# Sixteen instead of twelve row tiles of the down projection by seven products, weight low parts by adding DMA transfers, token-tile-major finish, and stacked rotary scores

## The chip, the cores and the metric

One core of a Trainium2 chip runs the whole program. The metric is device time in microseconds (us) of one execution; a measurement is the median of several. The engines named below are TensorE (PE: matrix products; its weight loads are a row of their own, PEld), VectorE (DVE), ScalarE (ACT), GpSimd (POOL), SyncE (SP, which here only issues DMA transfers), and the 16 DMA engines of the core.

## The reference

Two layers of a decoder on 512 tokens with 1024 features, all in float32. Per layer, with `swiglu(x) = (silu(x @ w_gate) * (x @ w_up)) @ w_down` and 2816 hidden columns:

```python
x = LN1(alpha * x + 0.5 * swiglu_1(x))
x = LN2(alpha * x + mixer(x))        # gated DeltaNet + conformer convolution + latent attention
x = LN3(alpha * x + 0.5 * swiglu_2(x))
```

The attention inside the mixer has four heads; a score is the sum of a part without position (128 wide) and a rotary part (64 wide, its key shared by the heads):

```python
s = (einsum('bqhd,bkhd->bhqk', q_nope[:, q0:q1], k_nope[:, :q1])
     + einsum('bqhr,bkr->bhqk', q_rope[:, q0:q1], k_rope[:, :q1])) * scale
```

## The kernel before

**Products in three passes.** A float32 matrix is split into a high part `h` (the value rounded to the type float32r, by a ScalarE copy) and a low part `lo = value - h` (by a VectorE subtraction): `split_into`. A product of two split matrices is three TensorE instructions, high by high, high by low and low by high (`mm3`). Products of two unsplit float32 matrices exist too, each of which appears in the trace as two instructions.

**Seven products instead of eight.** For a block product of two by two blocks the kernel uses a scheme with seven block products and some additions (`seven` for the gate and up projections, `seven_out` for the down projection). In the down projection the contraction has 22 row tiles of 128. `DOWN_FAST = 6` pairs of them (12 row tiles) go through `seven_out`: 7 products x 2 token tiles x 3 = 42 instructions of 512 columns a pair, where the direct way (`acc`) takes 2 x 8 x 3 = 48. `seven_out` walks over the pairs three times: a pass into the banks `x` and `y` (12 instructions a pair), one into `v`, `x`, `y` (18), one into `z`, `v` (12). The other 10 row tiles are done directly: a loop over the two halves of the output columns (`hf`), and in each over weights (`load`) and the four token tiles `tt` of 128 tokens; the last `TAIL = 5` weights of the second half are held, so that the token tiles end one after the other, 30 instructions apart. After its second half a token tile is normalised (`Norm.half`, `Norm.finish`), written out, and turned into the `xh`, `xl` of the next stage (`to_features`).

**Buffers.** Weights land in one of `RAWS = 5` buffers (`raw`), whose next load waits until its last reader is done; their split parts and sums of weights lie in slots, of which weights may hold 28 of 76.

**Order.** Each operation is recorded first, and `Planner.plan` then sets the order of all engines at build time from costs, due times (`prio`) and free buffers. On the chip each engine runs its list in that order and waits by semaphores.

**Rotary scores.** The rotary queries of two heads lie in one tile (`qr[h // 2]`), the shared key in two tiles, each with zeros in one half (`kropes`, two memsets by GpSimd). A score block of n columns is two unsplit float32 products, `qn` by `kn` and `qr` by `kropes`, with n = 128, 256, 384 and 512.

## Time and profile before

| | |
|---|---|
| runs | 2416.09, 2416.36, 2418.67 us; median 2416.36 |
| profiled execution | 2416.95 us, its span from the first to the last instruction 2415.2 us |
| busy | PE 2390.1, DVE 2215.7, ACT 1328.2, POOL 2.3 us |
| granted TensorE clock | 0.999 of full speed (2.4 GHz) |

A busy PE is not PE at its peak, since the end of a matmul is modelled; how densely it works is read from the count of matmuls of one shape in a stretch. The profile puts every operation on one line (288, the end of the planner), so operations are told apart by engine, shape and the names of what they write and read (`s` a slot, `ps` a bank of products, `raw` a weight buffer). The four down projections lie at about 226 to 353, 1098 to 1210, 1438 to 1551 and 2293 to 2406 us.

### The profile page before, as it was taken

The numbers are of one execution on the slowest core, as the hardware profiler recorded it, in microseconds if no ns is written. First come the engines' busy times: TensorE is split into PE (matmuls) and PEld (weight loads), VectorE is DVE, ScalarE is ACT, GpSimd is POOL, SyncE is SP. The second block draws the span as 40 slices with busy tenths as digits, with TensorE's granted clock in tenths as the row PEclk, the third lists the DMA queues.
The fourth block names the chain that finished last, engine by engine and source line by source line (L and its number), as shares of the span: only waits on it lengthen the run. The fifth ranks groups of instructions, "written<-read, shape, count | busy, mean of one in ns | idle before, by whom it ended". The sixth has DMA issues, their size and how long they took to land.

```text
span 2415.2 us, 41549 instructions
## 1 busy us (share of the span) xinstructions
PE 2390.1 (99%) x15716; PEld 2179.4 (90%) x15716; DVE 2215.7 (92%) x4559; ACT 1328.2 (55%) x2901; POOL 2.3 (0%) x8
## 2 busy tenths in 40 slices
PE   8999999999999999999999999999999999999998
PEld 8999888888899899998899998888888998999986
DVE  8998987999999799989799999789999997999896
ACT  6555538536746545656356565294376464555561
POOL 0000000000000000000000000000000000000000
PEclk9999999999999999999999999999999999999999
DMA  5334562412333623334523345523123335233451
GB/s 167 106 109 153 162 180 71 106 50 69 89 104 97 209 68 108 106 109 162 183 88 106 106 155 173 169 56 98 40 83 92 104 105 183 88 105 106 147 160 70
DMA packets 269833, 280.33 MB, mean 116 GB/s; under 512 B 18676, under 2 KB 221632, under 8 KB 269632
## 3 DMA queue, kind: packets, MB, share of 16 engines
q1 hardware_dynamic: 269632, 277.67, 38.3%
q8 instruction: 123, 2.02, 0.3%
q14 instruction: 78, 0.64, 0.1%
HBM read 260.33 MB, written 17.30 MB: 115 GB/s over the span
## 4 chain that ended last, share of the span: by engine, by line
PE 86%; DVE 7%; ACT 4%; DMA 1%; issue 1%; SPq 0%; DVEq 0%; ACTq 0%
PE ps L288 86%; DVE s L288 7%; ACT s L288 3%; ACT ps L288 1%; DMA raw<-in_ffn_w_up 0%; ACT xh L288 0%; DMA raw<-in_w_in 0%; DMA raw<-in_cv_w_pw 0%; DMA s<-in_x 0%; DMA raw<-in_ffn_w_gate 0%; DVE lny L288 0%; DVE xl L288 0%; DVE lnt L288 0%; DMA xspill<-s 0%; DVE cst L288 0%
## 5 line engine op out<-in xcount | busy, mean ns | idle before, releaser
L288 PE MATMUL ps<-s 128*128 128x256 f32 (+3 forms) x9068 | 1518.3, 323 | 1.4 <-DVE s L288 1.0
L288 PEld LDWEIGHTS ps<-s 128*128 128x128 f32 x9068 | 1324.9, 190 | 140.9 <-issue 5.7
L288 PE MATMUL ps<-xh,s 128*128 128x256 f32 (+2 forms) x4064 | 900.4, 307 | 1.5 <-ACT s L288 1.2
L288 DVE TENSOR_TENSOR s<-s 128x512 fp32r<-128x512 f32 (+9 forms) x1254 | 711.9, 600 | 4.3 <-ACT s L288 2.2
L288 PEld LDWEIGHTS ps<-xh,s 128*128 128x128 f32 (+1 forms) x4064 | 678.5, 190 | 34.8 <-ACT s L288 1.6
L288 PE MATMUL ps<-xl,s 128*128 128x256 f32 (+2 forms) x2032 | 624.6, 308 | 0.0
L288 DVE TENSOR_TENSOR s<-raw,s 128x512 fp32r<-128x512 f32 (+1 forms) x844 | 548.5, 679 | 11.9 <-ACT s L288 11.5
L288 ACT CAST s<-raw 128x512 fp32r<-128x512 f32 (+1 forms) x716 | 422.4, 619 | 220.7 <-DMA raw<-in_ffn_w_down 69.5
L288 ACT CAST s<-s 128x512 fp32r<-128x512 f32 (+1 forms) x786 | 436.3, 594 | 188.3 <-DVE s L288 179.1
L288 ACT COPY s<-ps 128x256 f32<-128x256 f32 (+3 forms) x664 | 257.2, 401 | 343.3 <-PE ps L288 336.1
L288 PEld LDWEIGHTS ps<-xl,s 128*128 128x128 f32 (+1 forms) x2032 | 387.0, 190 | 16.6 <-DVE xl L288 0.2
L288 DVE SCALAR_TENSOR_TENSOR s<-s 128x512 f32<-128x512 f32 (+26 forms) x356 | 249.9, 713 | 2.8 <-ACT s L288 2.1
L288 DVE TENSOR_TENSOR s<-ps,s 128x256 f32<-128x256 f32 (+1 forms) x336 | 147.4, 439 | 66.6 <-PE ps L288 53.8
L288 DVE TENSOR_TENSOR s<-raw 128x512 f32<-128x512 f32 x256 | 173.4, 682 | 5.1 <-issue 3.2
L288 ACT ACTIVATE s<-s 128x512 f32<-128x512 f32 x162 | 103.0, 666 | 59.6 <-DVE s L288 57.1
L288 PE MATMUL ps<-ident,s 128*128 128x128 f32 (+1 forms) x508 | 86.0, 277 | 12.6 <-DMA s<-in_x 5.0
L288 ACT CAST xh<-ps 128x512 fp32r<-128x512 f32 x48 | 28.6, 596 | 126.6 <-PE ps L288 126.6
L288 PEld LDWEIGHTS ps<-ident,s 128*128 128x128 f32 (+1 forms) x508 | 60.8, 142 | 32.2 <-issue 13.0
L288 DVE TENSOR_TENSOR s<-s,raw 128x512 f32<-128x512 f32 x128 | 87.2, 682 | 0.0
L288 DVE SCALAR_TENSOR_TENSOR s<-s,ps 128x512 f32<-128x512 f32 x96 | 63.4, 681 | 21.8 <-PE ps L288 18.9
L288 DVE TENSOR_TENSOR s<-s,ps 128x512 f32<-128x512 f32 x76 | 50.6, 680 | 32.4 <-PE ps L288 32.4
L288 ACT ACTIVATE s<-ps,s 128x512 f32<-128x512 f32 x58 | 40.3, 715 | 50.2 <-PE ps L288 50.2
(101 smaller groups left out, 599.3 us busy)
## 6 DMA issues: line engine op xcount, KB each, us to landing
raw<-in_w_in SPq DMA_DIRECT2D x106, 512.0 KB, 3.8
raw<-in_ffn_w_down SPq DMA_DIRECT2D x88, 512.0 KB, 4.4
raw<-in_ffn_w_gate SPq DMA_DIRECT2D x80, 512.0 KB, 3.8
raw<-in_ffn_w_up SPq DMA_DIRECT2D x80, 512.0 KB, 3.8
raw<-in_ffn_w_down SPq DMA_DIRECT2D x48, 256.0 KB, 2.6
spill<-s SPq DMA_DIRECT2D x40, 256.0 KB, 2.0
s<-spill SPq DMA_DIRECT2D x40, 256.0 KB, 4.7
raw<-in_w_out SPq DMA_DIRECT2D x16, 512.0 KB, 5.2
```

What stands on the lines that cost most here:

```text
L288: self.issued = o["f"](*o["a"], **o["k"])
```

## The change

In the down projections `DOWN_FAST` goes from 6 to 8 pairs (16 of 22 row tiles). The low part of a weight that came straight from memory is no longer subtracted by VectorE: ScalarE writes the negated value in float32r, and a GpSimd DMA adds the weight buffer to it (`split_adding`), for the first pass from pair `ADDING_FROM = 2` on, for all others and for the directly multiplied weights: 6 + 8 + 8 + 12 = 34 transfers of 256 KB in each down projection, 136 in all. Sums of weights (`t1`, `t3`, `t2`) are split as before. The directly multiplied rest is now a loop over token tiles outside and column halves inside, with all its weights held; the third pass leaves out the `v` products of the last `DOWN_LATE = 4` pairs, and these (`last`) come after token tile 1. The planner gets a cost for such a DMA. In the rotary scores, a query's split parts are stacked in the two halves of one tile per head, and the key's high and low part (each in both halves) are two float32r products of at least 256 columns.

```diff
+        if engine == "POOL" and name == "dma_start":
+            return 1200.0
...
+        if engine == "POOL" and name == "dma_start":
+            lat = 7000.0
...
-TAIL = 5
-DOWN_FAST = 6
+DOWN_FAST = 8
+DOWN_LATE = 4
+ADDING_FROM = 2
...
+        def split_adding(h, lo, part, src):
+
+            S.copy(h, part)
+            S.mul(lo, part, -1.0)
+            G.dma_start(out=lo.bitcast(F32), in_=src, accum_op=ADD)
...
-                split_into(h, lo, part)
+                if adding is None:
+                    split_into(h, lo, part)
+                else:
+                    split_adding(h, lo, part, part)
...
-            banks = seven_out(norm, wsrc, a32, fast) if fast else {}
+            if fast:
+                banks, last = seven_out(norm, wsrc, a32, fast, late)
+                norm.load()
+                rest = range(fast, n // 2)
+                ws = [[load(hf, fp, True) for fp in rest] for hf in range(2)]
+                for f in range(2 * fast, n):
+                    prepare(f)
+                for tt in range(NT):
+                    if tt == 2:
+                        last()
+                    for hf in range(2):
+                        old = (tt, hf) in banks
+                        ps = banks[tt, hf] if old else bank("dn")
+                        for fp, w in zip(rest, ws[hf]):
+                            for j in range(2):
+                                acc(ps, tt, 2 * fp + j, w, j, fp + j == fast and not old, old)
+                        norm.half(tt, hf, ps)
+                    norm.finish(tt)
+                return
...
-                product(x, halves(op, LO), wsplit(b11), i)
+                product(x, halves(op, LO), wsplit(b11, src if i >= ADDING_FROM else None), i)
...
-                product(y, s4, wsplit(b22), i, True)
+                product(y, s4, wsplit(b22, src), i, True)
...
-                t4 = slot(F32, WEIGHTS)
-                V.tensor_tensor(t4, b21, t2[i], op=SUB)
-                product(z, halves(op, LO), wsplit(b21), i)
-                product(v, halves(op, HI), wsplit(t4), i, True)
+                V.tensor_tensor(t2[i], b21, t2[i], op=SUB)
+                product(z, halves(op, LO), wsplit(b21, src), i)
+                if i < n - late:
+                    product(v, halves(op, HI), wsplit(t2[i]), i, True)
+                held.append(op)
+
+            def last():
+                for i in range(n - late, n):
+                    product(v, halves(held[i], HI), wsplit(t2[i]), i, True)
...
-            kr2 = slot()
-            G.memset(kr2[0:64], 0.0)
-            V.tensor_copy(kr2[64:128], krope[64:128])
-            G.memset(krope[64:128], 0.0)
-            kropes = krope, kr2
+            krope = split(rope(kr, swapped(kr_sb, (0, 0))))
...
-                qr.append(rope(t, swapped(ps, (0, 64))))
+                t = rope(t, swapped(ps, (0, 64)))
+                for i in range(2):
+                    q = slot(F32R)
+                    mine, other = slice(64 * i, 64 * i + 64), slice(64 - 64 * i, 128 - 64 * i)
+                    split_into(q[mine], q[other], t[mine])
+                    qr.append(q)
...
-                    PE.matmul(ps[:, 0:n], lhsT=qn[h][:, c], rhs=kn[h][:, 0:n], start=True, stop=False)
-                    PE.matmul(ps[:, 0:n], lhsT=qr[h // 2][:, c], rhs=kropes[h % 2][:, 0:n], start=False, stop=True)
+                    m = max(n, 256)
+                    for part in range(2):
+                        PE.matmul(ps[:, 0:m], lhsT=qr[h][:, c], rhs=krope[part][:, 0:m], start=part == 0, stop=False)
+                    PE.matmul(ps[:, 0:n], lhsT=qn[h][:, c], rhs=kn[h][:, 0:n], start=False, stop=True)
```

The change moves instructions at three places that matter below. The planner's end is line 288 before and line 292 after, so equal rows differ in that number.

ScalarE while the first down projection's first and second pass over the pairs are fed, before (`CAST s<-raw` is the high part of a loaded weight, `CAST s<-s` that of a sum or of hidden values):

```order
L288 CAST s<-s 128x512 x4
L288 CAST s<-raw 128x512
L288 CAST s<-s 128x512 x3
L288 CAST s<-s 128x256
L288 CAST s<-s 128x512
L288 CAST s<-raw 128x512
L288 CAST s<-s 128x512 x7
L288 CAST s<-s 128x256
L288 CAST s<-raw 128x512
```

The same engine at the same stage of the change:

```order
L292 CAST s<-raw 128x512
L292 ACTIVATE s<-raw 128x512
L292 CAST s<-s 128x512 x3
L292 CAST s<-s 128x256
L292 CAST s<-s 128x512
L292 CAST s<-s 128x256
L292 CAST s<-raw 128x512
L292 ACTIVATE s<-raw 128x512
L292 CAST s<-s 128x512 x2
```

Behind the cast of a loaded weight there is now a second pass over the same buffer, the negation (`ACTIVATE s<-raw`).

GpSimd's whole list from the last constant on, before:

```order
L1397 MEMSET const-bfloat16-1.0 128x1
L1397 MEMSET const-uint8-127 128x1
L1401 UNCONDITIONAL_BRANCH
L288 MEMSET s 64x512 x4
L1401 UNCONDITIONAL_BRANCH
L1397 ISA
```

and in the change:

```order
L1441 MEMSET const-bfloat16-1.0 128x1
L1441 MEMSET const-uint8-127 128x1
L1445 UNCONDITIONAL_BRANCH
L292 DMA s<-raw 128x512 x136
L1445 UNCONDITIONAL_BRANCH
L1441 ISA
```

The four memsets of the rotary keys are gone and 136 adding transfers have come, one behind the other in one queue that holds nothing else.

TensorE at the end of the first down projection and the start of the mixer, before (`ident,s 128x128` are the transposes that hand a normalised token tile to the next stage, `xh,s 72x256` is the first product of the mixer, `s 128x512` the down projection):

```order
L288 MATMUL ps<-s 128x512 x423
L288 MATMUL ps<-ident,s 128x128 x4
L288 MATMUL ps<-s 128x512
L288 MATMUL ps<-ident,s 128x128 x4
L288 MATMUL ps<-s 128x512 x33
L288 MATMUL ps<-ident,s 128x128 x4
L288 MATMUL ps<-s 128x512
L288 MATMUL ps<-ident,s 128x128 x4
L288 MATMUL ps<-s 128x512 x29
L288 MATMUL ps<-xh,s 72x256
```

and in the change:

```order
L292 MATMUL ps<-s 128x512 x433
L292 MATMUL ps<-ident,s 128x128 x4
L292 MATMUL ps<-s 128x512
L292 MATMUL ps<-ident,s 128x128 x4
L292 MATMUL ps<-s 128x512 x15
L292 MATMUL ps<-ident,s 128x128 x4
L292 MATMUL ps<-s 128x512
L292 MATMUL ps<-ident,s 128x128 x4
L292 MATMUL ps<-s 128x512 x23
L292 MATMUL ps<-xh,s 72x256
```

Behind the second token tile's last transposes there are now 23 instead of 29 instructions of the down projection, behind the first tile's 39 instead of 63. The two other tiles are handed over among the first products of the mixer: the third behind 35 of them, where it was behind 7.

## Rows read from the trace of the kernel before

**Rows 1.** The page's first part: busy us of each engine, its share of the span and its number of instructions.

```profile
PE 2390.1 (99%) x15716; PEld 2179.4 (90%) x15716; DVE 2215.7 (92%) x4559; ACT 1328.2 (55%) x2901; POOL 2.3 (0%) x8
```

**Rows 2.** The page's fourth part: the chain of work that ended last, its share of the span by engine.

```profile
PE 86%; DVE 7%; ACT 4%; DMA 1%; issue 1%; SPq 0%; DVEq 0%; ACTq 0%
```

**Rows 3.** The table of stretches: stretch, its length, then busy us (and instructions) of each engine, granted clock, share of the DMA engines, GB/s. The first three lie in the first layer's mixer, the fourth in a down projection, the fifth in a gate and up projection.

```profile
680.00:720.00 40.00, 40.00 (x287) 37.84 (x286) 40.00 (x70) 19.23 (x38) 0.00 (x0) 1.00 0.34 100
720.00:760.00 40.00, 39.50 (x268) 36.36 (x268) 38.27 (x81) 25.71 (x48) 0.00 (x0) 1.00 0.36 106
760.00:800.00 40.00, 40.00 (x293) 38.05 (x292) 37.55 (x67) 24.80 (x49) 0.00 (x0) 1.00 0.32 93
...
1120.00:1160.00 40.00, 40.00 (x178) 33.10 (x177) 40.00 (x69) 20.91 (x38) 0.00 (x0) 1.00 0.53 164
1360.00:1400.00 40.00, 40.00 (x336) 40.00 (x335) 35.55 (x64) 22.91 (x48) 0.00 (x0) 1.00 0.36 106
```

**Rows 4.** The timeline of the last down projection: start, us, engine, line, operation, count; in brackets the idle time before it and what ended that. The last two rows are the first and the last VectorE work behind the last matmul.

```profile
2344.64 61.36 PE L288 MATMUL ps<-s 128*128 128x512 f32 x270
...
2359.96 4.89 DVE L288 TENSOR_TENSOR s<-raw,s 128x512 fp32r<-128x512 f32 x8
...
2406.03 0.69 DVE L288 TENSOR_TENSOR s<-s,ps 128x512 f32<-128x512 f32 x1 [0.71 <-PE ps L288]
...
2410.70 1.41 DVE L288 SCALAR_TENSOR_TENSOR s<-s,lny 128x512 f32<-128x512 f32 x2
```

**Rows 5.** The timeline of TensorE in the mixer: unsplit float32 products (128 wide first, then score products of 384 and 512 columns) and what follows each.

```profile
540.88 14.90 PE L288 MATMUL ps<-s 128*128 128x128 f32 x132
555.53 0.48 PE L288 MATMUL ps<-xl,s 128*128 128x512 f32 x1
...
609.52 1.46 PE L288 MATMUL ps<-s 128*128 128x384 f32 x4
610.81 0.49 PE L288 MATMUL ps<-ident,s 128*128 128x128 f32 x3
611.14 1.88 PE L288 MATMUL ps<-s 128*128 128x512 f32 x4
612.86 0.60 PE L288 MATMUL ps<-ident,s 128*128 128x128 f32 x4
```

**Rows 6.** Groups of instructions with shapes kept apart: count, busy us in total, mean ns of one, idle us before them.

```profile
L288 DVE TENSOR_TENSOR s<-raw,s 128x512 fp32r<-128x512 f32 x700 | 459.3, 682 | 11.9 <-ACT s L288 11.5
...
L288 ACT CAST s<-raw 128x512 fp32r<-128x512 f32 x700 | 415.2, 622 | 219.0 <-DMA raw<-in_ffn_w_down 69.5 <-DMA raw<-in_w_in 43.9 <-DMA raw<-in_ffn_w_gate 38.5
...
L288 ACT ACTIVATE s<-s 128x512 f32<-128x512 f32 x162 | 103.0, 666 | 59.6 <-DVE s L288 57.1 <-DVE gu L288 1.8
...
L288 DVE TENSOR_TENSOR s<-s 128x256 f32<-128x256 f32 x100 | 38.4, 416 | 0.1
```

**Rows 7.** The page's sixth part: DMA issues with count, size of one and median us from issue to landing; and the landing times of all loads of the down projection's weights.

```profile
raw<-in_ffn_w_down SPq DMA_DIRECT2D x88, 512.0 KB, 4.4
...
raw<-in_ffn_w_down SPq DMA_DIRECT2D x48, 256.0 KB, 2.6
spill<-s SPq DMA_DIRECT2D x40, 256.0 KB, 2.0
s<-spill SPq DMA_DIRECT2D x40, 256.0 KB, 4.7
...
DMA to landing us min/median/max: 2.4/4.0/8.8
```

**Rows 8.** The table of stretches, as in rows 3, for the first down projection.

```profile
226.00:246.00 20.00, 20.00 (x140) 18.70 (x139) 17.38 (x33) 13.64 (x29) 0.00 (x0) 1.00 0.66 213
246.00:266.00 20.00, 20.00 (x90) 16.57 (x89) 20.00 (x37) 14.86 (x28) 0.00 (x0) 1.00 0.52 167
266.00:286.00 20.00, 19.04 (x85) 15.42 (x84) 20.00 (x36) 10.12 (x19) 0.00 (x0) 1.00 0.30 91
286.00:306.00 20.00, 20.00 (x90) 16.45 (x89) 19.50 (x35) 10.47 (x19) 0.00 (x0) 1.00 0.77 246
306.00:326.00 20.00, 20.00 (x90) 16.57 (x89) 15.33 (x27) 9.29 (x17) 0.00 (x0) 1.00 0.80 216
```

**Rows 9.** The waits of the DMA issuing queue of SyncE: who was waited for, us in total, times, longest.

```profile
SPq L288 <- DVE s L288: 1988.2, 485, 33.9
```

**Rows 10.** The timeline of TensorE where the down projections of the two first feed-forward blocks hand over to the mixers: every matmul that waited.

```profile
356.06 0.63 PE L288 MATMUL ps<-ident,s 128*128 128x128 f32 x4 [1.74 <-DVE s L288]
363.54 0.63 PE L288 MATMUL ps<-ident,s 128*128 128x128 f32 x4 [0.24 <-DVE s L288]
...
1553.91 0.63 PE L288 MATMUL ps<-ident,s 128*128 128x128 f32 x4 [0.33 <-DVE s L288]
1561.38 0.63 PE L288 MATMUL ps<-ident,s 128*128 128x128 f32 x4 [0.24 <-DVE s L288]
```

**Rows 11.** The chain of work that ended last, in order of time, in the first mixer: start, us, what (`cst` are the statistics of the convolution branch); and the wait of TensorE at its end.

```profile
593.09 100.99 PE ps L288 x611
...
734.96 1.22 DVE cst L288 x2
...
747.38 119.82 PE ps L288 x728
747.38 0.55 PE L288 MATMUL ps<-ident,s 128*128 128x128 f32 x3 [0.50 <-ACT s L288]
```

More of the change, by code (lines that the diff above doesn't have):

```diff
@@ L163, in _record @@
         lat = {"SP": 2000.0, "PE": 200.0, "ACT": 140.0, "DVE": 160.0, "POOL": 180.0}[engine]
+        if engine == "POOL" and name == "dma_start":
+            lat = 7000.0
         sb = [x for x in ins if x.space == bass.MemoryType.SB and (x.free_size() > 1 or outs[0].free_size() == 1)]
-        port = engine == "POOL" and bool(sb) or engine == "DVE" and (
+        port = engine == "POOL" and name != "dma_start" and bool(sb) or engine == "DVE" and (
             len(sb) > 1 or name in ("tensor_scalar", "tensor_copy") and len(sb) == 1 and outs[0].space == bass.MemoryType.SB)
@@ L407, in split_into, with weight @@
             (eng or V).tensor_tensor(lo, src, h.bitcast(F32), op=SUB)
-        def weight(shape, pieces, hold=False, biases=None):
+        def split_adding(h, lo, part, src):
+            S.copy(h, part)
+            S.mul(lo, part, -1.0)
+            G.dma_start(out=lo.bitcast(F32), in_=src, accum_op=ADD)
+        def weight(shape, pieces, hold=False, biases=None, adding=None):
             raw = pl.tile(wraw_p, shape, F32, "raw", RAWS)
@@ L429, in block, with wblock @@
             return src.rearrange("(k p) c -> p k c", p=128)
-        def wblock(src, hold=False):
+        def wblock(src, hold=False, adding=False):
             s = block(src)
-            return weight(list(s.shape), [(ALL, s)], hold)
+            return weight(list(s.shape), [(ALL, s)], hold, adding=s if adding else None)
         def wblock_first(src, i):
@@ L548, in trunk, with token_out @@
         LO, HI = slice(0, 256), slice(256, 512)
-        def token_out(norm, wsrc, n, ah, al, tail, prepare=None, a32=None, fast=0):
+        def token_out(norm, wsrc, n, ah, al, a32=None, fast=0, late=0, tail=0, prepare=None):
             def load(hf, fp, hold=False):
-                return wblock(wsrc[fp * 256:(fp + 1) * 256, hf * 512:(hf + 1) * 512], hold)
+                return wblock(wsrc[fp * 256:(fp + 1) * 256, hf * 512:(hf + 1) * 512], hold, fast > 0)
             def acc(ps, tt, f, w, j, first, more):
@@ L577, in token_out @@
                             f = n - 2 * rest + 2 * i + j
-                            acc(ps[tt], tt, f, w, j, f == 2 * fast and not old[tt], old[tt])
+                            acc(ps[tt], tt, f, w, j, f == 0, False)
                     norm.half(tt, hf, ps[tt])
@@ L581, in token_out, with seven_out @@
                         norm.finish(tt)
-        def seven_out(norm, wsrc, a32, n):
+        def seven_out(norm, wsrc, a32, n, late):
             pairs = [(i, n + i) for i in range(n)]
@@ L588, in rows, with wsplit @@
                 raw = pl.tile(wraw_p, [128, m], F32, "raw", RAWS)
-                Q.dma_start(out=raw, in_=wsrc[f * 128:(f + 1) * 128, cols])
-                return [raw[:, c:c + 512] for c in range(0, m, 512)]
-            def wsplit(w):
+                src = wsrc[f * 128:(f + 1) * 128, cols]
+                Q.dma_start(out=raw, in_=src)
+                return [(raw[:, c:c + 512], raw[:, c:c + 512]) for c in range(0, m, 512)]
+            def wsplit(w, src=None):
                 h, lo = slot(F32R, WEIGHTS), slot(F32R, WEIGHTS)
-                split_into(h, lo, w)
+                if src is None:
+                    split_into(h, lo, w)
+                else:
+                    split_adding(h, lo, w, src)
                 return h, lo
@@ L608, in seven_out @@
             for i, (f, g) in enumerate(pairs):
-                b11, b12 = rows(f)
+                (b11, src), (b12, _) = rows(f)
                 s = slot()
@@ L623, in seven_out @@
             for i, (f, g) in enumerate(pairs):
-                (b11, b12), (b22,) = rows(f), rows(g, slice(512, 1024))
+                (b11, _), (b12, _) = rows(f)
+                (b22, src), = rows(g, slice(512, 1024))
                 s = s23[i]
@@ L788, in ffn @@
             residual(src)
-            token_out(Norm(g[l], b[l], 4 * ALPHA, 16 * EPS, then), wd, NF, hh, hl, TAIL, prepare, hid, DOWN_FAST)
+            norm = Norm(g[l], b[l], 4 * ALPHA, 16 * EPS, then)
+            token_out(norm, wd, NF, hh, hl, hid, DOWN_FAST, DOWN_LATE, 0, prepare)
         def rope_setup():
@@ L1368, in mixer @@
             norm = Norm(a["ln2_g"][l], a["ln2_b"][l], 2 * ALPHA, 4 * EPS, "ffn")
-            token_out(norm, a["w_out"][l], 8, [m[0] for m in merged], [m[1] for m in merged], TAIL_OUT)
+            token_out(norm, a["w_out"][l], 8, [m[0] for m in merged], [m[1] for m in merged], tail=TAIL_OUT)
         for tt in range(NT):
```

15 lines of the change are left out of this document (6 added, 9 removed).

## The prediction

> **What bounds the kernel now.** First the busy times: PE 2390.1 of 2415.2 us, VectorE 2215.7, ScalarE 1328.2 [rows 1]. The chain that ended last is TensorE for 86% of the span and VectorE for 7% [rows 2], so TensorE is the bound and VectorE is close behind. A busy TensorE is not yet a dense one, so next the stretches: a down projection holds 178 matmuls of 512 columns in 40.00 us, a gate and up projection 336 of 256 columns [rows 3]. Over the whole last down projection it is 61.36 us for 270, 0.227 us each [rows 4], and 40.00 / 336 = 0.119 us for 256 columns. The spacing goes with the column count and nothing is left between: in these stages the time is the number of TensorE instructions, and an instruction less is time less, as long as VectorE, ScalarE and the transfers still deliver. VectorE is full there too, 20.00 of 20.00 us from 246 to 286 [rows 8], and in the mixer 40.00 of 40.00 [rows 3].
>
> **Down projection.** A pair through seven products costs 42 instructions instead of 48. Two more pairs in each of four down projections: 2 x 6 x 4 = 48 instructions fewer, 48 x 0.227 = **10.9 us**. All other products are moved, not changed.
>
> Whether the feeders keep up, per pair. By the code VectorE does, before, 4 full subtractions and 2 of 256 columns in the first pass, 6 and 3 in the second, 4 in the third. A full one takes 4.89 / 8 = 0.61 us [rows 4], a half one 38.4 / 100 = 0.38 us [rows 6]: 14 x 0.61 + 5 x 0.38 = 10.4 us, against 42 x 0.227 = 9.5 us of TensorE. For 8 pairs that is 83 against 76 us: without help VectorE would be late by some 7 us, minus what it has prepared. The change takes three full subtractions of each pair away (for two pairs, two): 8 x 10.4 - 22 x 0.61 = 70 us, below 76. ScalarE gets the negations. It then makes 13 full passes and one half pass a pair at 415.2 / 700 = 0.59 us [rows 6], about 8.0 us, below 9.5; up to 0.67 us each, the dearest such pass (`ACTIVATE`) [rows 6], it is 9.0 us. ScalarE is at 14.86 of 20 us in its fullest stretch there [rows 8]. So I put both at nothing, covered by TensorE's own 9.5 us a pair; without that cover it would be the 7 us above per down projection.
>
> **The adding transfer.** GpSimd was nearly idle (2.3 us [rows 1]), so no row shows a transfer issued there, nor one that adds. What stands behind it: its queue has only these 136, in the order in which ScalarE makes them ready; behind each landing wait TensorE's second product of three (high by low) and the reuse of the weight buffer. The second matters more, since SP's queue already spends 1988.2 us waiting for VectorE to let go of a buffer [rows 9], and now it waits for the landing instead. Call the time from issue to landing L. In the first pass a pair uses one of the five buffers and 12 x 0.227 = 2.72 us of TensorE; five make a turn of 13.6 us. The load takes 4.4 us [rows 7], cast and negation 1.2 us, which leaves L = 8.0 us before the ring sets the pace. In the third pass the load takes 2.6 us [rows 7], and 8 pairs use 4 x 2.72 + 4 x 1.36 = 16.3 us of TensorE, a mean turn of 10.2 us: L = 6.4 us. The second pass has two buffers per pair and 18 x 0.227 = 4.1 us, and leaves more. Bounds for L: 2.0 us, the shortest median of 256 KB (a store), and 8.8 us, the longest landing of any load of these weights [rows 7]. I take 4.7 us, that of the 256 KB loads which come in bunches [rows 7], since the adding transfers run between weight loads. Then nothing waits; at 8.8 us the two passes lose 8 x (5.6 + 8.8) / 5 - 21.8 + 8 x (3.8 + 8.8) / 5 - 16.3 = 5 us in each down projection, 20 us in all.
>
> The DMA engines: 213 GB/s at a share of 0.66 and 216 at 0.80 [rows 8] put a full engine set at some 300 GB/s (an estimate), so 256 KB cost 0.9 us once and 1.75 us if the read of the target counts too. 34 of them are 30 to 60 us in a stage of 480 x 0.227 = 109 us; the stage's own weights, now 15.7 MB, need 52 us. Together 82 to 112 us: it fits, at the upper end only just.
>
> **Finish by token tiles.** Before, TensorE waited 1.74, 0.24, 0.33 and 0.24 us for VectorE where the first feed-forward blocks hand over to the mixer [rows 10]. In the order now the third tile's transposes stand 35 products after the down projection's end instead of 7, 28 x 0.12 = 3.4 us later, and the last two tiles are 36 x 0.227 = 8.2 us apart, not 30 x 0.227 = 6.8. I take **2.0 us** of these 2.55; nothing if another wait comes instead, and at most 3 us. At the end of the kernel the tail stays: 2406.03 to 2410.70 and on [rows 4] hangs on the last matmul only.
>
> **Rotary scores.** An unsplit product shows as two instructions. 128 columns: (555.53 - 540.88) / 132 = 0.111, so 0.22 us a product; 384: (610.81 - 609.52) / 4 x 2 = 0.645; 512: (612.86 - 611.14) / 4 x 2 = 0.86 [rows 5]; 256, half of that, 0.43. A head drops 0.22 + 0.43 + 0.645 + 0.86 = 2.16 us, eight heads 17.3 us. New are two split products each of 256, 256, 384 and 512 columns: 2 x (0.12 + 0.12 + 0.17 + 0.227) = 1.27 us, for eight heads 10.2. That is **7.1 us** less for TensorE. VectorE gets four low parts of 64 rows and one of 128 a layer and loses a copy, about +2.7 us; ScalarE five casts, about 3 us, which its 19.23 of 40 us covers [rows 3]. VectorE has no cover in the mixer: it is full until 720, and the convolution's statistics at 734.96 end its run, after which TensorE waits 0.50 us [rows 11]. The planner's order answers that: counted in it with these durations, VectorE has 18.7 us more ahead of the statistics (gate work brought forward), and TensorE 18.2 us more ahead of the transposes that they need. So this wait grows by about 0.5 us a layer; I charge 1.0 us.
>
> **Sum**, against the profiled execution of 2416.95 us (span 2415.2): 2416.95 - 10.9 - 2.0 - 7.1 + 1.0 = 2397.95 us. The median of the runs lies 0.6 below that execution, which is less than I can tell: **2398 us**.
>
> **Rivals.** (a) *VectorE sets the mixer.* Its 2.7 us a layer come on top and the 7.1 us are waited away at the convolution: 2398 + 6.1 + 5.4 = 2409.5 us. For it: both engines are at 40.00 of 40.00 [rows 3]. Against: from 760 on VectorE has 2.45 us free in 40 [rows 3], and the order moves work into the gap.
>
> (b) *The adding transfers land late*, in the first and third pass. The loss per down projection is 3.2 x L - 23 us; it eats the 19 us gained at L = 8.7 us, and at L = 10 us it is 9 us, the kernel then 2398 + 36 = 2434 us. For it: loads of these weights took up to 8.8 us [rows 7], and the DMA engines come near to full. Against: 256 KB usually need 2.0 to 4.7 us.
>
> (c) *VectorE keeps GpSimd from issuing.* If a transfer could start only where VectorE pauses, and VectorE works 70 of 76 us, L would grow by several us, to the 2434 us of (b). For it: 20.00 of 20.00 us [rows 8]. Against: no row shows the two engines in each other's way. The Trainium skill (SBUF — State Buffer, Who interferes with whom) has such a lock: a VectorE copy or tensor_scalar in a two-port mode shuts GpSimd out of writing descriptors until it ends, while a subtraction of two buffers is said to clash with GpSimd's reads alone. By that page the subtractions that fill this stage would hold nothing up; no run here shows it yet.
>
> (d) *The gain is larger*: handovers and the mixer's starts lose their waits too, some 8 us more: 2390 us.
>
> **Chances.** The forecast (2390 to 2405 us) 0.62; (a), 2405 to 2411, 0.13; (d), below 2390, 0.05; (b) 0.15, of which 0.06 lies within no change and 0.09 above; (c) 0.05. A measurement tells apart 0.2%, 4.8 us. Faster than 2411.5 us: 0.62 + 0.13 + 0.05 = 0.80. The same: 0.06. Slower: 0.09 + 0.05 = 0.14. The range is 2389 to 2418 us, which leaves out about 0.05 below and 0.14 above; the likeliest case alone is 2390 to 2405.
>
> **What would show it.** Right: 178 matmuls in 40 us still within the down projections, and some 2.7 us less for each; landing of the GpSimd transfers at 3 to 6 us; score products at 0.12 to 0.23 us; the wait at the convolution below 2 us. Wrong: TensorE waiting in the down projection for a DMA with `s<-raw`; SP waiting for these transfers rather than for VectorE with the loads late behind; GpSimd's issues more than 2.7 us apart in the first pass; a VectorE chain ending in the convolution's statistics with a long TensorE wait behind it.

## The result and the profile after

The changed kernel takes 2450.36 us (median of 4 runs, 2442.59 to 2455.78), the kernel before beside it 2417.52: a ratio of 1.0130, 95% interval 1.0118 to 1.0143. The prediction was 2398 us; the change costs 33 us instead of gaining 19. The profiled execution lasts 2450.15 us, its span is 2448.4 (before 2415.2, [rows 1]).

The page's first part, its third (queue: packets, MB, share of 16 DMA engines), and one row of its sixth (DMA issues, median us to landing), of the kernel after:

```profile
PE 2393.4 (98%) x15668; PEld 2177.6 (89%) x15668; DVE 2188.0 (89%) x4535; ACT 1423.3 (58%) x3087; POOL 117.5 (5%) x140
...
q1 hardware_dynamic: 269888, 281.87, 38.1%
q0 software_dynamic: 19584, 35.66, 8.3%
...
s<-raw POOLq DMA_DIRECT2D x136, 256.0 KB, 6.2
...
PE 38%; DVE 7%; DMA 5%; ACT 2%; issue 1%; POOL 0%; DVEq 0%; SPq 0%; ACTq 0%; POOLq 0%
```

TensorE is still "busy" for 98%, and VectorE has lost work as planned (2215.7 to 2188.0). The chain of the work that ended last (last row, fourth part of the page) can be followed back only to 1156.8 us, so that its shares add up to 53% of the span: of that part TensorE has 38 in 53, or 72% (86% before, of a chain over nearly the whole span [rows 2]), and DMA, 1% before, has 5 in 53. GpSimd's queue takes 8.3% of the DMA engines' span: 8.3% of 2448.4 us by 136 is 1.49 us of all sixteen engines for one 256 KB adding transfer.

**Where the time went.** From the start times of the matmuls, the us from the first to the last product of 512 columns of each down projection, and of what lies between (a handover ends at the first product of 512 columns behind the mixer's 72 by 72 transposes):

| stretch | before | after | passes only | passes, ring of 7 |
|---|---|---|---|---|
| four down projections | 117.4, 116.2, 116.1, 114.2 | 130.5, 124.2, 126.9, 116.4 | 120.7, 117.2, 118.7, 113.4 | 122.2, 113.4, 113.8, 111.5 |
| handovers to the mixers | 21.9, 20.5 | 23.1, 20.0 | 19.9, 19.9 | 19.9, 20.0 |
| down to down of the next block | 224.7 | 225.2 | 223.8 | 224.4 |
| mixers, up to the next down | 720.3, 718.6 | 716.5, 721.1 | 718.1, 719.0 | 715.5, 716.4 |

The last two columns are experiments, below. In the changed kernel the down projections take 498.0 us for 463.9, where 480 products of 0.227 us would be 109 each. That is the whole loss (+34.1); the mixers give 1.3 back.

The table of stretches over the four down projections, kernel before, then after (stretch, length, busy us of PE, PEld, DVE, ACT, POOL with counts, granted clock, DMA share, GB/s):

```profile
226.00:353.00 127.00, 126.04 (x614) 106.16 (x613) 115.80 (x223) 67.19 (x125) 0.00 (x0) 1.00 0.60 181
1095.00:1220.00 125.00, 124.92 (x604) 105.02 (x603) 112.30 (x217) 63.07 (x118) 0.00 (x0) 1.00 0.48 155
1435.00:1560.00 125.00, 124.67 (x604) 104.95 (x603) 111.86 (x223) 60.33 (x115) 0.00 (x0) 1.00 0.57 172
2291.00:2406.00 115.00, 115.00 (x521) 95.43 (x519) 97.04 (x187) 45.76 (x86) 0.00 (x0) 1.00 0.38 120
```

```profile
226.00:353.00 127.00, 117.33 (x546) 97.44 (x545) 93.88 (x179) 82.62 (x157) 29.42 (x34) 0.96 0.97 241
1095.00:1220.00 125.00, 118.38 (x560) 98.51 (x559) 93.89 (x180) 82.66 (x157) 29.33 (x34) 0.97 0.95 246
1435.00:1560.00 125.00, 118.83 (x601) 100.29 (x600) 90.04 (x159) 84.37 (x162) 29.28 (x34) 0.99 0.93 233
2291.00:2406.00 115.00, 112.25 (x622) 97.98 (x621) 93.89 (x166) 81.45 (x158) 25.87 (x30) 0.99 0.86 225
```

In the first one the DMA engines were at 0.60 and are at 0.97. In us of all engines: 0.60 x 127 = 76 before, and 34 x 1.49 = 51 more make 127 of 127. The losses (13, 8, 11 and 2 us) stand in the order of the shares before: the fourth down projection had 0.38 (no next block's weights are loaded beside it), and it lost least. That the full average is itself the cause does not follow; an experiment below speaks against it.

Within the first one, ten us at a time, after:

```profile
266.00:276.00 10.00, 10.00 (x46) 8.28 (x45) 6.86 (x13) 5.93 (x12) 1.72 (x2) 1.00 0.83 239
...
296.00:306.00 10.00, 9.94 (x44) 8.25 (x45) 10.00 (x18) 7.13 (x13) 3.04 (x5) 1.00 1.01 256
306.00:316.00 10.00, 6.95 (x28) 5.06 (x27) 5.87 (x10) 6.57 (x13) 4.31 (x6) 0.96 1.01 264
316.00:326.00 10.00, 4.44 (x14) 3.18 (x13) 0.00 (x0) 1.18 (x3) 1.66 (x2) 0.84 1.10 271
326.00:336.00 10.00, 9.82 (x31) 7.85 (x32) 0.32 (x1) 6.59 (x13) 5.16 (x6) 0.69 1.13 231
336.00:346.00 10.00, 10.00 (x46) 8.29 (x45) 7.42 (x13) 3.97 (x8) 0.00 (x0) 1.00 1.16 270
```

(The share sums the packets that begin in a stretch, so it can pass 1.00.) Up to 306 TensorE is nearly dense (41 to 46 products in 10 us from 246 on). Then, in the third pass and ahead of the late weight blocks (those of the directly multiplied rest, six of 512 KB), TensorE and ScalarE stop, and VectorE has nothing to do (0.00 and 0.32 us): no engine is the bound, the transfers are. Before it can issue the next load, SP's queue waited for VectorE there (104.3 us from 280 to 400 in the kernel before); now it waits about as long for landings as for VectorE (us in total, times, longest):

```profile
SPq L292 <- DVE s L292: 41.9, 15, 16.9
SPq L292 <- DMA s<-raw: 40.6, 13, 5.9
```

The stop also costs clock: from 316 to 326 TensorE worked for 4.44 us, and from 326 to 336 it is busy again, but at a granted 0.69 (a mean of its two levels, 1.2 and 2.4 GHz) it makes 31 products for 46.

The chain in the second down projection, in order of time (start, us, what):

```profile
1169.39 6.73 DMA raw<-in_ffn_w_down
...
1176.70 14.44 DMA raw<-in_ffn_w_down
...
1192.69 0.83 POOL s L292
...
1193.70 7.09 DMA s<-raw
...
1200.91 0.37 SPq L292
...
1201.33 4.90 DMA raw<-in_ffn_w_gate
```

The load of a late block, 512 KB, whose like took 4.4 us before [rows 7], stands in the chain for 14.44; its low part is then added in 7.09, and only behind that landing does SP issue loads of the next block's weights. The engines in between show it too (ScalarE's timeline: its first cast of the late block ahead of that one, then its first cast of that one, each with the idle time before it):

```profile
1187.79 0.62 ACT L292 CAST s<-raw 128x512 fp32r<-128x512 f32 x1 [7.37 <-DMA raw<-in_ffn_w_down]
...
1191.22 0.62 ACT L292 CAST s<-raw 128x512 fp32r<-128x512 f32 x1 [1.24 <-DMA raw<-in_ffn_w_down]
```

### The profile page after: what moved, and what is told of

It is laid out like the page before. It is cut to its first block, busy times and chain, and to the rows that moved or that the text cites. A ratio compares the mean times of both kernels' runs of the same rounds, so it can differ in the third digit from the quotient of the medians.

```text
span 2448.4 us, 42105 instructions
## 1 busy us (share of the span) xinstructions
PE 2393.4 (98%) x15668; PEld 2177.6 (89%) x15668; DVE 2188.0 (89%) x4535; ACT 1423.3 (58%) x3087; POOL 117.5 (5%) x140
## 3 DMA queue, kind: packets, MB, share of 16 engines
q1 hardware_dynamic: 269888, 281.87, 38.1%
q0 software_dynamic: 19584, 35.66, 8.3%
## 4 chain that ended last, share of the span: by engine, by line
PE 38%; DVE 7%; DMA 5%; ACT 2%; issue 1%; POOL 0%; DVEq 0%; SPq 0%; ACTq 0%; POOLq 0%
PE ps L292 38%; DVE s L292 6%; ACT s L292 2%; DMA raw<-in_ffn_w_down 2%; DMA raw<-in_w_in 1%; DMA s<-raw 1%; DMA raw<-in_ffn_w_gate 0%; DMA raw<-in_w_out 0%; ACT ps L292 0%; DMA raw<-in_ffn_w_up 0%; DMA raw<-in_dn_w_o 0%; DVE st L292 0%; POOL s L292 0%; DVE lny L292 0%; DVE lnt L292 0%
## 5 line engine op out<-in xcount | busy, mean ns | idle before, releaser
L292 PE MATMUL ps<-s 128*128 128x256 f32 (+2 forms) x9020 | 1518.1, 324 | 28.3 <-ACT s L292 13.8
L292 DVE TENSOR_TENSOR s<-s 128x512 fp32r<-128x512 f32 (+9 forms) x1344 | 757.6, 598 | 4.8 <-ACT s L292 1.3
L292 ACT CAST s<-raw 128x512 fp32r<-128x512 f32 x708 | 423.4, 620 | 264.1 <-DMA raw<-in_w_in 71.5
L292 ACT CAST s<-s 128x512 fp32r<-128x512 f32 (+1 forms) x844 | 466.8, 591 | 163.6 <-DVE s L292 155.1
L292 DVE TENSOR_TENSOR s<-raw,s 128x512 fp32r<-128x512 f32 (+1 forms) x708 | 459.8, 678 | 21.9 <-ACT s L292 21.3
L292 DVE SCALAR_TENSOR_TENSOR s<-s 128x512 f32<-128x512 f32 (+27 forms) x356 | 250.9, 713 | 1.8 <-ACT s L292 0.9
L292 POOL DMA_DIRECT2D s<-raw x136 | 117.3, 865 | 2295.3 <-ACT s L292 2228.7
L292 DVE TENSOR_TENSOR s<-raw 128x512 f32<-128x512 f32 x272 | 184.5, 682 | 16.1 <-DMA raw<-in_ffn_w_down 7.5
L292 DVE TENSOR_TENSOR s<-s,raw 128x512 f32<-128x512 f32 x136 | 92.6, 681 | 0.0
L292 ACT ACTIVATE s<-raw 128x512 fp32r<-128x512 f32 x136 | 85.3, 627 | 0.0
```

Of the source, the lines that this page charges most:

```text
L292: self.issued = o["f"](*o["a"], **o["k"])
```

## The experiments

All are timed against the kernel before on the same chip.

| run | us | ratio (95%) |
|---|---|---|
| changed kernel | 2450.4 | 1.0130 (1.0118 to 1.0143) |
| stacked scores alone | 2415.2 | 0.9989 (0.9980 to 0.9997) |
| changed, no adding transfer | 2428.9 | 1.0043 (1.0031 to 1.0055) |
| adding in the passes only | 2417.1 | 0.9993 (0.9983 to 1.0002) |
| adding in the late blocks only | 2463.5 | 1.0188 (1.0175 to 1.0201) |
| passes only, finish by halves | 2426.4 | 1.0038 (1.0025 to 1.0050) |
| changed, seven raw buffers | 2435.4 | 1.0076 (1.0063 to 1.0088) |
| changed, plain transfers | 2411.6 | 0.9978 (0.9968 to 0.9988) |
| adding in passes one and two | 2419.7 | 1.0016 (1.0006 to 1.0026) |
| scores, no more VectorE work | 2419.1 | 1.0006 (0.9997 to 1.0015) |
| **passes only, seven raw buffers** | **2404.6** | **0.9949 (0.9936 to 0.9963)** |
| passes one and two, seven buffers | 2420.9 | 1.0015 (1.0006 to 1.0024) |
| scores alone, seven buffers | 2422.3 | 1.0016 (1.0008 to 1.0025) |
| scores, casts on GpSimd | 2416.0 | 0.9993 (0.9984 to 1.0002) |
| passes only, seven, casts on GpSimd | 2404.8 | 0.9950 (0.9937 to 0.9962) |
| passes only, six buffers | 2416.1 | 0.9994 (0.9985 to 1.0003) |

### Which part of the change costs

Stacked scores alone: the three hunks of the change in the mixer, put into the kernel before.

> Only the stacked rotary scores are put into the kernel before; its down projections stay as they were. My step on the scores: TensorE drops 17.3 us of plain products and gets 10.2 us, the wait at the convolution grows by 1.0: 6 us less, 2411 us. Rival: in the changed kernel the two mixers together are only 1.3 us shorter (720.3 to 716.5 and 718.6 to 721.1 us), so most of the 7 us is waited away elsewhere in the mixer: 2416 us, no change that can be measured.

2415.2 us, 2.7 us less (interval 0.7 to 4.8). Nearer to the rival: what is missing is taken up below.

No adding transfer (the first of these places serves the late blocks, the second the three passes):

```diff
-                return wblock(wsrc[fp * 256:(fp + 1) * 256, hf * 512:(hf + 1) * 512], hold, fast > 0)
+                return wblock(wsrc[fp * 256:(fp + 1) * 256, hf * 512:(hf + 1) * 512], hold)
...
-                if src is None:
-                    split_into(h, lo, w)
-                else:
-                    split_adding(h, lo, w, src)
+                split_into(h, lo, w)
```

> The changed kernel, with every low part subtracted on VectorE again; 8 pairs through seven products and the finish by token tiles stay. Theory A, the adding transfers fill the DMA engines (share 0.97 over the down projection, 0.6 before) and the loads are late for it: the DMA share falls back to about 0.65, no load of these weights takes 15 us, and the four down projections fall from 124 us on average to about 113 (240 matmuls-of-two by 0.227 is 109) plus up to 7 us where VectorE is late: 2405 to 2430 us. Theory B, the finish by token tiles needs all six late weight blocks at once and loses the time whoever makes the low parts: the down projections stay at 120 us and more, 2440 us or above.

2428.9 us, the DMA share over the first down projection is back at 0.58: theory A, but not down to a gain. VectorE is full again (9.4 to 9.8 of 10 us a stretch), and the down projections take 128.7, 116.1, 119.0 and 113.8 us, together 14 more than before.

The two halves of that edit, each alone:

> The changed kernel with VectorE subtracting the low parts of the six late weight blocks (12 transfers of 34 less in each down projection); the three passes keep theirs. Theory A: 12 x 1.5 us of full DMA engines are taken out just where loads took 15 us, VectorE has room there (it is idle for 20 us from 316 to 336): most of the 45 us of waits go, 2405 to 2420 us. Theory B: the waits stay, only their releaser changes to VectorE: 2440 us or above.

> The other half: VectorE subtracts in the three passes, the six late weight blocks keep their 12 adding transfers. Theory A: 22 x 1.5 us of DMA time go, loads run ahead again, but the 12 transfers still meet the last loads and the next stage's: between the kernel without any and the changed one, 2415 to 2435 us, with some 5 us a down projection lost to VectorE in the passes. Theory B: 2440 us or above.

2417.1 and 2463.5 us. The effects add: from 2428.9 the transfers of the passes gain 12 us, those of the late blocks cost 35, together 2452 (measured 2450.4). So 22 of 34 transfers do what they were made for, and 12 do all the damage: they come when the six late blocks, the third pass's rows and the next block's first weights are loaded at once. In the run with the late ones alone the transfer lands in 7.8 us, in that without them in 5.8. My range for "late ones alone" (2415 to 2435) was wrong: I took the loss to grow with the number of transfers, and it depends on where they stand.

That run also parts the crowded place from the average. Its first down projection, as a whole, then two of its ten-us slices, then pieces of its chain from 290 to 360 (start, us, what):

```profile
226.00:353.00 127.00, 116.07 (x548) 94.90 (x546) 105.91 (x197) 72.76 (x135) 10.47 (x12) 0.99 0.70 194
...
294.00:304.00 10.00, 9.56 (x41) 7.25 (x41) 10.00 (x19) 2.88 (x6) 0.00 (x0) 1.00 0.17 53
...
324.00:334.00 10.00, 9.35 (x34) 7.55 (x35) 0.00 (x0) 6.56 (x12) 4.49 (x6) 0.83 1.11 259
```

```profile
289.77 18.57 DVE s L292 x33
...
320.42 9.28 DMA s<-raw
...
329.83 12.26 DMA raw<-in_w_in
```

The DMA engines are at 0.70 on the whole, not full, and its four down projections are the longest of all (133.5, 130.5, 127.3 and 122.0 us). VectorE, full in the passes, lets go of the buffers late, and meanwhile the DMA engines lie nearly idle (0.17). Then everything is loaded at once (1.11), a late transfer stands in the chain for 9.28 us, and the next block's load behind it for 12.26.

### Is it the finish by token tiles?

The run with adding in the passes only, given the finish of the kernel before (left half for four token tiles, then the right half, three blocks held; all of the third pass ahead of it).

> The run with adding in the three passes only, and the finish of the kernel before: first the left half of the columns for all four token tiles, its late weights one block after the other, then the right half with three blocks held. All products of the third pass come before it. Theory B: with the finish by token tiles all six late blocks (3 MB) are wanted at once while the third pass is still loading; by halves they are wanted three at a time over some 33 us, so the gap at 304 to 324 (3.5 us of TensorE in the first down projection) goes, and with it most of the 30 us by which the four down projections exceed 480 x 0.227 = 109 us each: 2390 to 2405 us. Theory C: VectorE comes late out of the second pass and sets the third one whatever follows: 2412 to 2422 us.

2426.4 us, 9 us more than by token tiles: theory B falls. The down projections are a little shorter (467.1 us in all for 470.0), but what lies behind them is longer: handovers 22.5 and 25.4 us for 19.9 and 19.9, and 227.3 for 223.8. The finish by token tiles is worth more than I gave it.

### What makes the transfers dear

Seven raw buffers in the changed kernel, and the 136 transfers without the addition:

```diff
-RAWS = 5
-N_SLOTS = 76
+RAWS = 7
+N_SLOTS = 72
```

> The changed kernel with seven raw weight buffers for five (four of 76 other buffers less). Theory A, the DMA engines are full: more loads in flight move no more bytes, 2445 to 2455 us. Theory D, the ring: the adding transfer holds a raw buffer until it lands (SP waits 40.6 us for these landings from 280 to 400 us), the next load starts late, and two more buffers give 2 / 5 of the slack back: 2420 to 2435 us.

```diff
-            G.dma_start(out=lo.bitcast(F32), in_=src, accum_op=ADD)
+            G.dma_start(out=lo.bitcast(F32), in_=src)
```

> The changed kernel, in which the 136 transfers copy the weight into the low part instead of adding it (the negation beneath is overwritten, so the low parts are wrong). It measures what the adding itself costs. If adding doubles the work of the DMA engines, a transfer falls from 1.49 us of all 16 engines (8.3% of 2448 us by 136) to about 0.87 us (what 256 KB of a load cost: 38.1% of 2448 us for 281.87 MB), the share over a down projection from 0.97 to 0.8, and the time by half of the loss or more: 2415 to 2430 us. If the adding is free and it is the source in SBUF or the queue that makes them dear: share and time as before, 2445 to 2455 us.

2435.4 and 2411.6 us. The larger ring gives 15 us back while the first down projection's DMA share stays full (0.99): against theory A, by which more loads in flight would change nothing, and at the end of theory D's range (2420 to 2435). Plain transfers, which leave out the addition, give 39 us back, more than the 33 that the change lost and more than I expected (2415 to 2430). The page's third and sixth part, one group of GpSimd's instructions (busy us, mean ns, idle us and what ended it) and the first down projection's stretch, with plain transfers; then the same group of the changed kernel:

```profile
q0 software_dynamic: 10880, 35.66, 3.9%
...
s<-raw POOLq DMA_DIRECT2D x136, 256.0 KB, 4.6
...
L292 POOL DMA_DIRECT2D s<-raw x136 | 73.3, 539 | 2299.5 <-ACT s L292 2251.7 <-DVE s L292 19.4 <-PE ps L292 13.6
...
226.00:353.00 127.00, 124.40 (x595) 104.02 (x594) 102.64 (x200) 88.14 (x168) 18.43 (x34) 0.99 0.78 255
```

```profile
L292 POOL DMA_DIRECT2D s<-raw x136 | 117.3, 865 | 2295.3 <-ACT s L292 2228.7 <-DVE s L292 28.3 <-PE ps L292 26.7
```

The same bytes go in 10880 packets instead of 19584 and take 3.9% instead of 8.3% of the engines: 0.69 us of all sixteen for 256 KB instead of 1.49. Adding makes a transfer 2.2 times as dear for the engines, and 1.6 times as dear to issue on GpSimd (865 for 539 ns). With them at 0.78 instead of 0.97, the loads keep up. The plain transfer is cheaper in three ways at once, for the engines, to issue and until it lands (4.6 for 6.2 us); which of the three counts for how much of the 39 us was not tried.

The Trainium skill (DMA: Bandwidth & Descriptors, Anatomy of one DMA — SWDGE (gpsimd) path) fits a transfer issued by GpSimd by 2.0 us and its bytes over 436 GB/s, an estimate of 2.6 us for 256 KB. Here the plain ones land in 4.6 us and the adding ones in 6.2 us among other traffic, both later than by that fit.

### Where the adding may stay

Passes one and two only (VectorE subtracts in the third pass and for the late blocks), then with seven raw buffers; and the three passes with seven and with six buffers:

> Adding transfers only in the first and second pass (14 in each down projection); VectorE subtracts in the third pass and for the six late blocks, finish by token tiles. Theory A: 8 x 1.5 = 12 us of DMA time less while the loads bunch, and VectorE has 4 x 0.61 = 2.4 us of work for 2.7 us of TensorE a pair in the third pass: 2403 to 2413 us. Theory C, VectorE is already late out of the second pass and has no time to give: 2417 to 2427 us.

> Adding transfers in the first and second pass only (2420 us with five raw buffers), seven raw buffers. Here the transfers are over when the late loads bunch, so the ring has only loads: if loads wait for raw buffers, 2403 to 2412 us; if it is VectorE that comes late out of the second pass, 2416 to 2422 us.

> The run with adding in the three passes only (2417 us), with seven raw buffers for five (72 other buffers for 76). Its TensorE still waits for landings in the third pass (two waits of 1.9 and 0.55 us in the first down projection, SP waits 21.4 us for landings there). If the ring is what makes the loads late, they go: 2400 to 2410 us. If the DMA engines are (share 1.0 from 284 to 324), nothing changes: 2414 to 2420 us.

> Adding in the three passes only with six raw buffers (74 other buffers): between five, 2417 us, and seven, 2405 us. If the ring sets how far the loads run ahead, 2408 to 2413 us; if the seventh buffer's gain was an accident of the planned order, the time can fall outside the two.

2419.7, 2420.9, **2404.6** and 2416.1 us. Where the third pass has no transfers, the ring changes nothing and VectorE sets the pace (three waits, 4.8 us, in the second down projection). Where it has them, two buffers more take 12.5 us away, as I expected if the ring makes the loads late, and not if the DMA engines do: a transfer holds its raw buffer until it lands, and the next load stands in line behind it. Waits of SP's queue from 280 to 330 (us in total, times, longest), with five buffers and with seven:

```profile
SPq L292 <- DMA s<-raw: 21.4, 9, 6.6
```

```profile
SPq L292 <- DMA s<-raw: 14.7, 6, 3.2
```

And waits of TensorE. In the second down projection and a little more, 1093 to 1240, the changed kernel has these, and the version with seven buffers and adding in the passes only has none:

```profile
PE ps L292 <- DMA s<-raw: 2.7, 2, 2.5
PE ps L292 <- ACT s L292: 2.1, 1, 2.1
PE ps L292 <- DVE s L292: 1.8, 1, 1.8
```

In the third, with adding in the passes only, five buffers (1480 to 1556) and then seven (1430 to 1592, the longest of its waits):

```profile
PE ps L292 <- DMA s<-raw: 3.0, 2, 2.0
```

```profile
PE ps L292 <- ACT s L292: 0.4, 1, 0.4
```

Six buffers came out at five's level (2416.1 for 2417.1 us), outside my range for a ring that sets the pace (2408 to 2413): its runs lie from 2408 to 2421 us, so that the size of the step from six to seven is not settled. Seven buffers by themselves are no gain:

> The kernel before with the stacked scores and seven raw buffers, without any adding transfer: is the larger ring by itself worth something? In the run of the changed kernel with seven buffers, the stretches between the down projections were 4 to 5 us shorter as well. If loads are late there for want of a buffer, 2403 to 2410 us; if that came from fewer adding transfers behind the handover only, 2413 to 2417 us as the scores alone.

2422.3 us, 7 us more than the scores alone with five, and outside both of my ranges. Its trace has the loss in the down projections (473.5 us in all for 464.7) and not in the mixers. That the four other buffers which the ring displaces are missed there is likely but was not shown. In the runs here the ring pays only where adding transfers hold it.

### Why the scores gave so little

VectorE's new work replaced by ScalarE copies; then the opposite, ScalarE's casts moved to GpSimd:

```diff
-                    split_into(q[mine], q[other], t[mine])
+                    G.tensor_copy(q[mine], t[mine])
+                    V.tensor_tensor(q[other], t[mine], q[mine].bitcast(F32), op=SUB)
```

> The kernel before with the stacked scores alone, and in them ScalarE copies where VectorE subtracted the low parts (so the low parts of rotary queries and keys are wrong): VectorE has nothing more to do than before. The scores alone gave 2.7 us where I forecast 6. Rival (a) of the prediction, VectorE's 2.7 us a layer come on top: without them the gain is there, 2410 to 2412 us. The other way, the freed TensorE time is waited away at places that VectorE's extra work does not set: 2414 to 2416 us, as with it.

> The kernel before with the stacked scores alone; the four casts of rotary queries a layer, 64x512, 0.615 us each on ScalarE, go to GpSimd. Theory E: ScalarE is full in the stretch of the scores (38.92 of 40 us from 580 to 620, 35.80 before) and its new casts push the exponentials and copies that TensorE waits for: 2.5 us a layer less there, most of the missing 3.4 us is back, 2410 to 2413 us. Rival: the freed TensorE time is lost to the planner's order, whoever casts: 2414 to 2417 us.

> The run with adding in the passes and seven raw buffers (2404.6 us), and these four casts a layer on GpSimd. Theory E: 2400 to 2403 us. Rival: 2404 to 2407 us, as without.

2419.1, 2416.0 and 2404.8 us. Without VectorE's extra work it is 4 us slower, but that run puts as many passes on ScalarE instead (39.01 of 40 us from 580 to 620), so it does not clear VectorE; and moving four of ScalarE's casts a layer away brings nothing either. The stretch of the first layer's scores, 580 to 620, in the kernel before, with the scores alone, and with the casts on GpSimd; and a wait of TensorE in the second layer, with the scores alone:

```profile
580.00:620.00 40.00, 39.06 (x183) 29.48 (x182) 38.47 (x108) 35.80 (x96) 0.52 (x1) 1.00 0.44 135
```

```profile
580.00:620.00 40.00, 39.06 (x192) 30.25 (x191) 38.59 (x108) 38.92 (x104) 0.00 (x0) 1.00 0.30 95
...
1790.06 0.33 PE L288 MATMUL ps<-ident,s 128*128 128x128 f32 x1 [1.59 <-ACT s L288]
```

```profile
580.00:620.00 40.00, 38.83 (x194) 30.59 (x192) 38.77 (x107) 36.87 (x99) 8.48 (x4) 1.00 0.42 131
```

ScalarE, the fourth figure, is nearly full exactly where the scores are: 35.80 of 40 us before and 38.92 with the new casts, and TensorE waits for it (1.59 us). With the casts on GpSimd ScalarE has 2 us back, but the four casts take 8.48 us there, 2.1 on average, and they differ widely. The third and the fourth in the first layer (GpSimd's timeline), then what VectorE does beside them:

```profile
593.71 5.84 POOL L288 CAST s<-s 64x512 fp32r<-64x512 f32 x1 [2.00 <-DVE rky L288]
...
599.61 0.61 POOL L288 CAST s<-s 64x512 fp32r<-64x512 f32 x1
```

```profile
596.59 2.49 DVE L288 TENSOR_TENSOR s<-raw,s 128x512 f32<-128x512 f32 x4
599.00 1.40 DVE L288 SCALAR_TENSOR_TENSOR s<-ps,s 128x512 f32<-128x512 f32 x2
```

The long one lasts as long as a run of nine VectorE operations that each read two buffers; it ends once VectorE reads products (`ps`) instead, and beside such an operation the next takes 0.61 us, as long as on ScalarE. The second layer has the same pair (5.85 and 0.61; GpSimd's spans are rough). So this run did not simply relieve ScalarE: it also made one cast a layer late.

In that run the spacing of the matmuls beyond its usual value (the run's median for the same two shapes, where it is exceeded by more than 0.05 us) grew behind the scores, where the convolution joins: 2.5 us for 1.9 with the scores alone (680 to 800) and 2.2 for 0.8 (1880 to 2000), while in the second layer's scores it fell (8.8 for 10.1, 1750 to 1880). So ScalarE's load is seen, but that it is the cause was not shown: where it was relieved, the time was lost one place further.

## Why the prediction was wrong, step by step

**What bounds the kernel: right**, and where nothing waits the count of products is the time: 46 products in 10 us, 480 for 492 in each down projection. Two of the signs that the prediction named for being wrong came: TensorE waits in each down projection for a DMA with `s<-raw` (3.0, 2.7, 4.4 and 2.8 us), and SP waits for landings where it waited for VectorE, with loads late behind.

**The step that failed: the transfers of the late blocks had no term.** For the adding transfers the prediction says "Then nothing waits". I worked out the ring for the first and the third pass, and none of it for the 12 transfers of the six late blocks, which were so put at nothing without a reason. They cost 33 us in the changed kernel (2450.4 for 2417.1 without them) and 35 where they are the only ones (2463.5 for 2428.9).

**What let it pass: the DMA engines' budget.** The prediction said of the adding transfers and the weights "Together 82 to 112 us: it fits, at the upper end only just"; 112 is already more than the stage's 109. The price of a transfer was bounded rightly, 0.9 to 1.75 us; it is 1.49. The other term was wrong: 52 us for the stage's own weights alone, where the row of the same stretch shows 76 us of use by all traffic (next block's weights, norm parameters, stores). 76 + 51 is 127 of 127 us, full. But the average does not decide: with the late transfers alone it is 0.70 and the kernel is slowest, with seven buffers it is 0.99 and 15 us are back. What the average hides is that the loads bunch at the end of the stage, beside transfers that hold their buffers.

**Landing time.** I took 4.7 us (bounds 2.0 and 8.8); the median is 6.2, that of the 22 in the passes 5.6, that of the 12 late ones 7.9, and the longest took 12.9. By my formula 3.2 x 6.2 - 23 is below zero, no loss. The formula held the loads at 2.6 and 4.4 us; one stood in the chain for 14.44, beside transfers on the same engines. Of rival (b), "the adding transfers land late", effect and sign came true, by another way than it gave: not in the first and third pass, but at the late blocks, where the loads and the landings are late together.

**Rival (c), VectorE keeps GpSimd from issuing: no.** An issue takes 865 ns on average, the same 0.86 us where VectorE is full and where it stands still, and in all GpSimd has 4.5 us of waits without a releaser. Two issues, where VectorE is at 10.00 and at 0.32 of 10 us, and GpSimd's waits (total, times, longest):

```profile
249.50 0.86 POOL L292 DMA_DIRECT2D s<-raw  x1 [2.88 <-ACT s L292]
...
332.39 0.86 POOL L292 DMA_DIRECT2D s<-raw  x1 [0.17 <-issue]
...
POOL s L292 <- issue: 4.5, 25, 0.2
```

The lock that the Trainium skill (SBUF — State Buffer, Who interferes with whom) describes for VectorE's copies was not put to the test: beside the 136 issues VectorE ran no copy and a single tensor_scalar. That the subtractions of this stage would hold nothing up by that page agrees with the trace: GpSimd's waits of the last row are 0.2 us at most.

**VectorE at nothing: near.** Without any adding transfer the four down projections take 13.9 us more than before although 10.9 us of products are gone, so some 25 us are lost, 14 of them in the first: 6 each on average, near the 7 that the prediction named as the price without help. With adding in the passes and seven buffers they take 460.9 us, 8 more than the forecast's 453, nearly all of it one wait for VectorE (below).

**Finish by token tiles, 2.0 us: too small, the sign right.** With adding in the passes only, handovers and the next block's start are 2.0, 0.6 and 0.9 us shorter than before, 3.4 in all; against the old finish with the same eight pairs it is 9 us. In the changed kernel, with its late loads, the three are 1.3 us longer than before.

**Scores, 7.1 us less 1.0.** Measured alone 2.7. I covered ScalarE's casts with its 19.23 of 40 us, which is the row of another stretch (680 to 720, [rows 3]); where the casts fall it is 35.80. In the version with seven buffers and adding in the passes the mixers are 4.8 and 2.2 us shorter than before, 7.0 together: the forecast's size. The ring has a part in it: in three pairs of runs that differ in seven buffers for five, the two mixers are shorter by 2.4 us (the scores alone), 5.2 (adding in the passes only) and 6.4 (the changed kernel). No run has seven buffers without the scores, so how much of it is the scores' is open.

**In sum** that version takes 2404.6 us, 0.5% below the kernel before and 1.9% below the changed one: mixers -7.0, handovers and the next block's start -2.8, down projections -2.9. Three of its down projections are near what the forecast made of them, 2.2 to 2.8 us less than before (113.4, 113.8, 111.5); only the first takes 122.2 us for 114.7, 7.5 us more, about as much as the version lies above 2398. It has one wait of TensorE that the others lack (from 232 to 358):

```profile
PE ps L292 <- DVE s L292: 6.5, 1, 6.5
```

Why there alone was not tried.

## What to carry over

Before a transfer is added, take the DMA engines' share over that very stretch from the trace, all queues counted, and look at it in slices of ten us: an average says little when the loads bunch at the end of the stretch, as the run with 0.70 and the longest down projections shows. A cover for new work has to be read from the stretch in which the work falls, not from a neighbour. And where a transfer holds the buffer into which the next load goes, count the buffers together with it: here the same 22 transfers gave nothing with five and 12 us with seven.

## What the runs showed of the hardware

A transfer that adds from SBUF to SBUF uses packets of half the size (19584 for 10880 packets of the queue for the same 35.66 MB) and 1.49 us of all sixteen engines for 256 KB, a plain one 0.69, the same bytes on SP's queue 0.87 on average (38.1% of 2448.4 us for 281.87 MB). GpSimd needs 865 ns to issue it, whether VectorE is full or idle, and 539 for a plain one. Where loads and adding transfers meet (a DMA share of 1.0 to 1.1), one load of 512 KB stood in the chain for 14.44 us where 4.4 was usual. And GpSimd's cast of 64x512 took from 0.61 us, as on ScalarE, to 5.85 us beside VectorE operations that read two buffers.
